# All 128 up blocks ahead of the first down block, in a fused decoder layer on one core

## The chip, the core and the metric

The kernel runs on one core of a Trainium2 chip. The core's engines work side by side, each through its own list of instructions in order: TensorE (PE) multiplies matrices, VectorE (DVE) and ScalarE (ACT) work element by element, GpSimd (POOL) issues the gathers here, and SyncE (SP) issues most of the other transfers between the chip's memory (DRAM) and the core's. ACT issues some transfers too. All transfers run on the same 16 DMA engines. The metric is the device time of one execution in microseconds (us).

## The reference, cut to what matters

The layer takes 512 tokens of width 1024 through a modulation, two kinds of attention with a projection, a LayerNorm, a PEER feed-forward part and a last LayerNorm. The change touches the PEER part alone, which is this:

```python
q = (hx @ w_pq).reshape(PEER_CHUNK, PEER_HEADS, 2, PEER_HALF)
sc = jnp.einsum('thpd,hpnd->thpn', q, sub_keys)
v_half, i_half = lax.top_k(sc, PEER_TOPK)          # 16 of 128 keys, twice per head
cand = v_half[:, :, 0, :, None] + v_half[:, :, 1, None, :]
cand_idx = i_half[:, :, 0, :, None] * N_KEYS + i_half[:, :, 1, None, :]
top_s, top_pos = lax.top_k(cand.reshape(...), PEER_TOPK)
idx = jnp.take_along_axis(cand_idx, top_pos, axis=-1)
g = jax.nn.softmax(top_s, axis=-1)
a = jax.nn.gelu(jnp.einsum('thkd,td->thk', u_tab[idx], hx), approximate=False)
return jnp.einsum('thk,thkd->td', (g * a).astype(hx.dtype), v_tab[idx])
```

Each token picks 8 x 16 of 16384 experts. An expert has a row of 1024 in `u_tab` and one in `v_tab`.

## The kernel before, in words

Tokens 0 to 127, and the first 64 tokens of the second tile for their `u` rows, go through **gathers**: POOL fetches one row of a table per token (`fetch`, L741, 512 KB for 128 rows), DVE multiplies it with the hidden row and sums (`dot`, L746), or adds a weighted `v` row to an accumulator (L782). There are 64 + 128 fetches of `u` and 128 of `v`, with five buffers. The generators `gather_part` and `gather_tile` hand out these steps, and a function `pull` takes steps worth so many nominal microseconds per block.

The rest of the tokens are computed **densely**, over 128 blocks of 128 experts. An **up block** (`u_block`, L802) loads 512 KB of `u`, splits it into a high part on ACT (L86) and a low part on DVE (L87), runs 24 matmuls over 320 tokens (L96 to L98 with the name `st`) and takes a GELU on ACT (L812). The result, `[128, 320]`, stays in a ring of 32 buffers (`a_r`) or goes to DRAM (`a_s`, then `a_d`, written by a transfer that ACT issues, L817) and is loaded again by SP later (`a_b`, L871). A **down block** (`v_block`, L858) loads 512 KB of `v`, splits it in the same way, multiplies the activation with the gate values of its experts (L874 on ACT, L875 on DVE), splits the product (L880, L881) and runs 18 matmuls of 512 columns into six accumulators in PSUM (L96 to L98 with the name `acc`).

**Gates.** Dense gate values come from the chosen indices: `make_g` builds one-hot tiles on DVE (L682, L684), scaled copies on ACT (`go`, L688), 8 small matmuls per step on PE in two groups of four (L692), and two copies of the PSUM results into a stage tile (L695), one on ACT and one on DVE. Two such steps fill a 1 MB stage that SP writes to `g_d` (L699). There are 48 steps for three tiles of 128 tokens. The down blocks read them back, 8 blocks at a time (`gl`, 1.5 MB, L853, issued by ACT, two buffers).

**Order.** Ahead of the gates comes the selection itself (`topk`, L553 to L660), also spread over the up blocks on DVE. The first loop runs `NB + NS` up blocks: `NB` = 32 kept in the ring and `NS` spilled to DRAM. In each of them some top-k work is pulled, `GRATE` gate steps are drained, and gather steps worth `RA` (before the weights of the second tile are ready) or `RB` (after) are pulled. The second loop runs 128 down blocks; as long as up blocks are left, each of its rounds runs one first and pulls 3.6 us of gather steps, afterwards 1.9 us. The down blocks take ring activations first, then the later up blocks' and the spilled ones last (`order`). At round 112 of 128 the ring is closed and the last stage's constants and inputs are loaded (L906 to L911); at round 116 the rest of the gathers is flushed. A scheduler places the instructions of each engine from this program order, so neighbouring blocks overlap and loads move ahead. Gather arithmetic is tied to the low-part splits by order (`paced`), so it can't run ahead of them.

SP's list is in order: a load that waits for a free buffer (three of `raw`) holds up all transfers behind it. The program also gives each transfer of SP and ACT one of eight completion counters (DMAHW0 to DMAHW7 in the order), in turn, and a transfer that gets a counter waits until the counter's last transfer has landed.

## Time and profile before

| | us |
|---|---|
| median of 3 runs | 1595.51 (1591.92 to 1604.62) |
| the profiled execution | 1601.17 |
| its span in the profile | 1599.4 |

| engine | busy us | share of the span |
|---|---|---|
| PE (matmul) | 1459.3 | 91% |
| DVE | 1309.6 | 82% |
| ACT | 782.3 | 49% |
| POOL | 486.7 | 30% |

The transfers moved 438.30 MB, 274 GB/s over the span. The mean granted TensorE clock was 0.959 of full speed. A busy share is an average over stages, so it is read per stage: the block loops' first weight split starts on DVE at 351.3 us, the 43rd at 640.75 us, the first product of a down block is made at 846.61 us, the last matmuls of an up block start at 1185.3 us, and the last gather step starts at 1443.84 us and takes 1.28 us.

### The profile page before, as it was taken

What the parts mean: (1) busy time and instruction counts of PE and PEld (TensorE: products, weight loads), DVE (VectorE), ACT (ScalarE), POOL (GpSimd) and SP (SyncE); (2) the same over time, 40 slices, a digit from 0 to 9 for tenths busy, and PEclk for the clock granted to TensorE, in tenths of its full rate; (3) what the DMA queues carried; (4) which work ended last, traced back from release to release, by engine and by line L of the source; (5) the groups of instructions that cost most, each with busy time, mean ns of one, the idle gap of its engine ahead of it and who ended that gap; (6) DMA issues with size and microseconds to landing.
All of it is one profiled execution on the core that took longest, in us unless ns stands there. A gap on an engine that the chain in (4) does not pass through costs nothing.

```text
span 1599.4 us, 22711 instructions
## 1 busy us (share of the span) xinstructions
PE 1459.3 (91%) x7837; PEld 1272.5 (80%) x7837; DVE 1309.6 (82%) x2654; ACT 782.3 (49%) x1475; POOL 486.7 (30%) x338
## 2 busy tenths in 40 slices
PE   6999898998688888999998989999999997899996
PEld 5777776888677778899997879999988885678884
DVE  7897665999899899988966888898889895778566
ACT  2565533335256668898963434443343342334340
POOL 0000000000543333752224655565545563430000
PEclk9999898999898899999998999999999997999998
DMA  8855443222877678998999999999989999998751
GB/s 303 290 189 186 152 165 112 79 80 80 302 252 254 229 259 297 316 365 319 326 366 341 368 365 363 366 368 378 364 315 369 349 352 353 334 336 268 225 174 53
DMA packets 173334, 438.30 MB, mean 274 GB/s; under 512 B 14562, under 2 KB 79458, under 8 KB 170019
## 3 DMA queue, kind: packets, MB, share of 16 engines
q1 hardware_dynamic: 69666, 234.72, 41.2%
q0 software_dynamic: 46080, 167.79, 29.0%
q10 hardware_dynamic: 57472, 34.35, 7.3%
q8 instruction: 61, 1.00, 0.2%
q14 instruction: 55, 0.44, 0.1%
HBM read 397.45 MB, written 39.33 MB: 273 GB/s over the span
## 4 chain that ended last, share of the span: by engine, by line
PE 49%; DMA 14%; issue 14%; DVE 13%; POOL 4%; ACT 4%; SPq 0%; POOLq 0%; DVEq 0%; ACTq 0%
DMA gl<-g_d 7%; PE acc L97 7%; PE acc L98 7%; PE acc L96 7%; PE bank L96 4%; PE bank L97 4%; PE bank L98 4%; POOL gb L741 4%; PE st L98 3%; PE st L96 3%; PE st L97 3%; DVE lo L87 2%; PE acc L692 2%; DMA gb<-u_tab,ei 2%; DVE gb L746 2%
## 5 line engine op out<-in xcount | busy, mean ns | idle before, releaser
L86 ACT CAST hi<-raw 128x1024 fp32r<-128x1024 f32 x286 | 299.2, 1050 | 278.5 <-DMA raw<-v_blk 71.8
L87 DVE TENSOR_TENSOR lo<-raw,hi 128x1024 fp32r<-128x1024 f32 x286 | 348.0, 1219 | 80.7 <-ACT hi L86 79.0
L96 PE MATMUL st<-h2h,hi 128*128 128x320 f32 x1024 | 330.5, 323 | 33.0 <-ACT hi L86 33.0
L98 PE MATMUL st<-h2h,lo 128*128 128x320 f32 x1024 | 328.3, 321 | 23.0 <-DVE lo L87 22.8
L97 PE MATMUL st<-h2l,hi 128*128 128x320 f32 x1024 | 325.3, 318 | 0.0
L97 PE MATMUL acc<-lo,wh 128*128 128x512 f32 x768 | 306.1, 399 | 17.6 <-DVE lo L87 17.0
L96 PE MATMUL acc<-hi,wh 128*128 128x512 f32 x768 | 304.3, 396 | 11.3 <-ACT hi L86 11.1
L98 PE MATMUL acc<-hi,wl 128*128 128x512 f32 x768 | 303.4, 395 | 0.0
L741 POOL DMA_INDIRECT gb<-u_tab,ei x128 | 204.1, 1595 | 229.0 <-DVE gb L746 213.0
L746 DVE SCALAR_TENSOR_TENSOR gb<-gb,h2n 128x1024 f32<-128x1024 f32 x192 | 231.0, 1217 | 17.3 <-DMA gb<-u_tab,ei 9.6
L741 POOL DMA_INDIRECT gb<-v_tab,ei x128 | 183.9, 1437 | 193.2 <-DVE acc L782 176.3
L96 PEld LDWEIGHTS st<-h2h,hi 128*128 128x128 f32 x1024 | 200.5, 196 | 39.0 <-ACT hi L86 37.3
L98 PEld LDWEIGHTS st<-h2h,lo 128*128 128x128 f32 x1024 | 199.6, 195 | 29.1 <-DVE lo L87 28.9
L97 PEld LDWEIGHTS st<-h2l,hi 128*128 128x128 f32 x1024 | 200.1, 195 | 1.5
L97 PEld LDWEIGHTS acc<-lo,wh 128*128 128x128 f32 x768 | 147.0, 191 | 52.2 <-DVE lo L87 21.4
L688 ACT ACTIVATE go<-oh,iT 128x128 f32<-128x128 bf16 x384 | 169.0, 524 | 33.9 <-DVE oh L682 26.9
L96 PEld LDWEIGHTS acc<-hi,wh 128*128 128x128 f32 x768 | 147.0, 191 | 43.5 <-ACT hi L86 12.8
L741 POOL DMA_INDIRECT gb<-u_tab,eip x64 | 88.8, 1387 | 280.3 <-DVE cand L555 148.7
L98 PEld LDWEIGHTS acc<-hi,wl 128*128 128x128 f32 x768 | 147.2, 192 | 30.9
L782 DVE SCALAR_TENSOR_TENSOR acc<-gb,w,acc 128x1024 f32<-128x1024 f32 x127 | 162.3, 1278 | 2.1 <-DMA gb<-v_tab,ei 2.0
L880 ACT CAST wh<-w 128x384 fp32r<-128x384 f32 x128 | 65.4, 513 | 177.1 <-PE acc L97 106.6
L104 POOL TENSOR_TENSOR rs_r<-rs_v,mhalf 128x1 f32<-128x1 f32 (+1 forms) x12 | 9.3, 775 | 399.8 <-DVE rs_v L102 364.2
(214 smaller groups left out, 2049.4 us busy)
## 6 DMA issues: line engine op xcount, KB each, us to landing
raw<-u_T SPq DMA_DIRECT2D x128, 512.0 KB
raw<-v_blk SPq DMA_DIRECT2D x128, 512.0 KB
wada<-w_adaT SPq DMA_DIRECT2D x48, 512.0 KB
g_d<-stage SPq DMA_DIRECT2D x24, 1024.0 KB
gl<-g_d ACTq DMA_DIRECT2D x16, 1536.0 KB
a_d<-a_s ACTq DMA_DIRECT2D x56, 160.0 KB
a_b<-a_d SPq DMA_DIRECT2D x56, 160.0 KB
raw<-w_pqT SPq DMA_DIRECT2D x16, 512.0 KB
```

What stands on the lines that cost most here:

```text
L86: nc.scalar.copy(hi, src)
L87: split.last = nc.vector.tensor_sub(lo, src, hi.bitcast(F32))
L96: nc.tensor.matmul(ps, lh, rh, start=first, stop=False)
L97: nc.tensor.matmul(ps, lh, rl, start=False, stop=False)
L98: nc.tensor.matmul(ps, ll, rh, start=False, stop=last)
L104: nc.gpsimd.tensor_tensor(r, v, mhalf.to_broadcast([P, n]), op=OP.pow)
L688: nc.scalar.activation(go[:, i, :], oh0[:, :, i], AF.Copy, scale=iT[:, 2, t0 + i:t0 + i + 1])
L692: nc.tensor.matmul(ps[:, i * P:(i + 1) * P], oh1[:, 4 * u + i, :], go[:, 4 * u + i, :], start=True, stop=True)
L741: nc.gpsimd.indirect_dma_start(out=b, out_offset=None, in_=A[tab], in_offset=bass.IndirectOffsetOnAxis(ap=idx[:, j:j + 1], axis=0))
L746: paced(nc.vector.scalar_tensor_tensor(b, b, 1.0, h2n, op0=OP.mult, op1=OP.mult, accum_out=acc))
L782: paced(nc.vector.scalar_tensor_tensor(acc0, b, w0[:, j:j + 1], acc0, op0=OP.mult, op1=OP.add))
L880: nc.scalar.copy(wh, w)
```

## The change

The first loop runs all 128 up blocks (`NB + NS` = 128), with 96 activations instead of 56 by way of DRAM; the second loop runs down blocks alone. `GRATE` falls from 0.8 to 0.52 gate steps per up block, `RA` from 2.2 to 1.7, `RB` rises from 1.3 to 1.9, and a down block's gather steps go from 3.6 (beside an up block) or 1.9 us to 1.6 us. Both stage copies of a gate step are on ACT. The tile for reloaded activations has four buffers instead of two.

```diff
-NS = 56
-GRATE = 0.8
+NS = 96
+GRATE = 0.52
...
-RA = 2.2
-RB = 1.3
+RA = 1.7
+RB = 1.9
...
-                    (nc.scalar.copy if u == 0 else nc.vector.tensor_copy)(
+                    nc.scalar.copy(
                         stage[:, :, w:w + 4].rearrange("p i t -> p t i"), ps.rearrange("p (t i) -> p t i", t=4))
...
-            a = vp.tile([P, TU], F32, name="a_b", tag="a_b", bufs=2)
+            a = vp.tile([P, TU], F32, name="a_b", tag="a_b", bufs=4)
             dma(a, a_d[e - NB])
...
             u_block(n + NB + NS)
             c2 = pull(gt, c2 + 3.6)
         else:
-            c2 = pull(gt, c2 + 1.9)
+            c2 = pull(gt, c2 + 1.6)
```

DVE, in the up blocks where top-k and gate steps overlap. Before (`lo` is a weight split, `gb,dots` a gather product, `oh` the one-hot tiles, `eq` top-k work, `stage` the PSUM copy):

```order
L645 TENSOR_TENSOR eq<-ab,lev 128x2048
L682 TENSOR_TENSOR oh_4857<-iTb,iota_3470 128x1024
L648 TENSOR_TENSOR eq<-eq,ixx 128x2048
L684 TENSOR_TENSOR oh_4859<-iT,iota 128x1024
L746 SCALAR_TENSOR_TENSOR gb,dots_3801<-gb,h2n 128x1024 x2
L695 COPY stage<-acc 128x4x128
L87 TENSOR_TENSOR lo<-raw,hi 128x1024
L651 TENSOR_TENSOR eq<-eq 128x8x128
L682 TENSOR_TENSOR oh_4925<-iTb,iota_3470 128x1024
L651 TENSOR_TENSOR eq<-eq 128x8x64
L684 TENSOR_TENSOR oh_4927<-iT,iota 128x1024
```

The same engine in the changed kernel, also in the up blocks with top-k and gate steps (`tv`, `tp`, `cand` are top-k work):

```order
L682 TENSOR_TENSOR oh_4524<-iTb,iota_3510 128x1024
L684 TENSOR_TENSOR oh_4526<-iT,iota 128x1024
L746 SCALAR_TENSOR_TENSOR gb,dots_3841<-gb,h2n 128x1024
L87 TENSOR_TENSOR lo<-raw,hi 128x1024
L553 MAX tv<-cand 128x8
L746 SCALAR_TENSOR_TENSOR gb,dots_3841<-gb,h2n 128x1024
L554 MAX_INDEX tp<-tv,cand 128x8
L87 TENSOR_TENSOR lo<-raw,hi 128x1024
L555 MATCH_REPLACE cand<-tv,cand 128x80
L682 TENSOR_TENSOR oh_4648<-iTb,iota_3510 128x1024
```

The copy from PSUM is gone from DVE, a gate step comes with about every second split, and fewer products stand between two splits. Counted between the first and the 43rd split of the block loops: 64 products, 20 gate steps and 19 copies before; 51, 14 and none now. The last gather step stands after 223 splits before (128 up and 95 down blocks) and after 232 now (128 and 104).

ACT, where gate steps meet spilled up blocks (`hi` is a weight's high part, `a_s` the GELU result, `a_d` its transfer to DRAM). Before:

```order
L688 ACTIVATE go<-oh_7914,iT 128x128 x8
L86 CAST hi<-raw 128x1024
L812 ACTIVATE a_s<-st 128x320
L695 COPY stage<-acc 128x4x128
L817 DMA a_d_125<-a_s 128x320
L688 ACTIVATE go<-oh_7976,iT 128x128 x8
L86 CAST hi<-raw 128x1024
```

ACT in the changed kernel:

```order
L688 ACTIVATE go<-oh_6673,iT 128x128 x5
L812 ACTIVATE a_s<-st 128x320
L86 CAST hi<-raw 128x1024
L817 DMA a_d_108<-a_s 128x320
L695 COPY stage<-acc 128x4x128 x2
L688 ACTIVATE go<-oh_6777,iT 128x128 x7
L812 ACTIVATE a_s<-st 128x320
L86 CAST hi<-raw 128x1024
L817 DMA a_d_109<-a_s 128x320
```

Both copies of a gate step now stand in ACT's list, where each waits for PE's small matmuls.

SP at the end of the gate steps (`raw` is a block's weights, `a_b` a reloaded activation, `g_d` a full stage). Before:

```order
L699 DMA g_d<-stage 128x2048
L92 DMA raw<-u_T 128x1024
L871 DMA a_b<-a_d_83 128x320
L871 DMA a_b<-a_d_84 128x320
L92 DMA raw<-u_T 128x1024 x5
L92 DMA raw<-v_blk 128x1024
L92 DMA raw<-u_T 128x1024
```

SP in the changed kernel:

```order
L699 DMA g_d<-stage 128x2048
L92 DMA raw<-u_T 128x1024
L871 DMA a_b<-a_d_83 128x320
L871 DMA a_b<-a_d_84 128x320
L871 DMA a_b<-a_d_85 128x320
L871 DMA a_b<-a_d_86 128x320
L92 DMA raw<-u_T 128x1024 x11
L92 DMA raw<-v_blk 128x1024 x33
L906 DMA g2r<-g_d 128x1024
```

Before, loads of `u` and `v` take turns from here on, for 40 rounds; now the last 11 `u` loads stand together and 33 `v` loads follow. The other 92 reloads of activations come one for about each later `v` load.

## Rows read from the trace of the kernel before

**Rows 1.** Windows by stage: stretch and length, then busy us (instructions) of each engine.

```profile
core 0: us, PE busy (x) PEld busy (x) DVE busy (x) ACT busy (x) POOL busy (x), PEclk, DMA share, GB/s
351.30:640.70 289.40, 236.99 (x1400) 217.74 (x1399) 266.16 (x738) 174.77 (x294) 94.32 (x68) 0.92 0.68 234
640.70:819.80 179.10, 175.09 (x1269) 171.54 (x1269) 160.65 (x202) 165.34 (x326) 73.45 (x41) 1.00 0.93 335
...
878.10:1183.70 305.60, 297.72 (x1630) 268.46 (x1629) 262.81 (x354) 121.32 (x201) 166.54 (x115) 0.99 0.98 360
1183.70:1311.00 127.30, 126.92 (x565) 105.08 (x564) 116.80 (x136) 50.76 (x90) 73.52 (x49) 1.00 0.99 359
1311.00:1445.10 134.10, 113.70 (x441) 89.20 (x440) 97.75 (x116) 42.33 (x75) 49.62 (x35) 0.89 0.96 339
1445.10:1599.40 154.30, 140.24 (x613) 114.50 (x612) 99.81 (x149) 51.55 (x93) 2.20 (x4) 0.97 0.56 177
```

**Rows 2.** Windows again, the whole stretch between two of those borders.

```profile
640.70:1445.10 804.40, 762.47 (x4216) 682.67 (x4216) 672.51 (x849) 399.48 (x721) 382.44 (x253) 0.97 0.97 350
```

**Rows 3.** Groups by line: operation, shapes, count, busy us, mean ns, idle before.

```profile
L86 ACT CAST hi<-raw 128x1024 fp32r<-128x1024 f32 x286 | 299.2, 1050 | 278.5 <-DMA raw<-v_blk 71.8 <-PE bank L97 71.0 <-PE st L97 50.7
L746 DVE SCALAR_TENSOR_TENSOR gb<-gb,h2n 128x1024 f32<-128x1024 f32 x192 | 231.0, 1217 | 17.3 <-DMA gb<-u_tab,ei 9.6 <-DMA gb<-u_tab,eip 5.9 <-issue 1.6
L684 DVE TENSOR_TENSOR oh<-iT,iota 128x1024 f32<-128x1024 f32 x48 | 58.3, 1214 | 0.0
L695 DVE COPY stage<-acc 128x512 f32<-128x512 f32 x48 | 50.7, 1056 | 18.2 <-PE acc L692 18.1
L682 DVE TENSOR_TENSOR oh<-iTb,iota 128x1024 bf16<-128x1024 bf16 x48 | 32.6, 682 | 4.3 <-ACT go L688 4.2
L812 ACT ACTIVATE a_s<-st 128x320 f32<-128x320 f32 x56 | 24.2, 434 | 16.1 <-PE st L98 8.8 <-DMA g_d<-stage 7.3
```

**Rows 4.** DMA queues: SP's (q1), POOL's (q0), ACT's (q10).

```profile
q1 hardware_dynamic: 69666, 234.72, 41.2%
q0 software_dynamic: 46080, 167.79, 29.0%
q10 hardware_dynamic: 57472, 34.35, 7.3%
```

**Rows 5.** Timeline of PE in an up block and in a down block.

```profile
750.11 0.31 PE L98 MATMUL st<-h2h,lo 128*128 128x320 f32 x1
...
752.45 0.31 PE L96 MATMUL st<-h2h,hi 128*128 128x320 f32 x1
...
1299.75 0.39 PE L96 MATMUL acc<-hi,wh 128*128 128x512 f32 x1
...
1300.88 0.39 PE L98 MATMUL acc<-hi,wl 128*128 128x512 f32 x1
```

**Rows 6.** Chain of waits: start, us, what; one gate step, one load of gates.

```profile
493.11 1.80 PE acc L692 x16
...
1309.91 29.56 DMA gl<-g_d
```

**Rows 7.** Windows again, two of 40 or 80 us.

```profile
720.00:800.00 80.00, 79.15 (x565) 76.71 (x564) 70.64 (x88) 74.22 (x149) 18.52 (x16) 1.00 0.89 323
1160.00:1200.00 40.00, 40.00 (x209) 35.32 (x209) 33.08 (x37) 16.58 (x28) 17.52 (x13) 1.00 0.88 315
```

**Rows 8.** Page, 40 slices of the span: what the DMA engines moved.

```profile
GB/s 303 290 189 186 152 165 112 79 80 80 302 252 254 229 259 297 316 365 319 326 366 341 368 365 363 366 368 378 364 315 369 349 352 353 334 336 268 225 174 53
```

**Rows 9.** Timeline of DVE: the wait for the first load of gates.

```profile
846.61 0.49 DVE L875 TENSOR_TENSOR w<-a_r,gl 128x320 f32<-128x320 f32 x1 [15.69 <-DMA gl<-g_d]
```

**Rows 10.** Waits of SP's queue from 1183 to 1445 us: total, times, longest.

```profile
SPq L911 <- DMA gl<-g_d: 21.9, 1, 21.9
SPq L92 <- DMA gl<-g_d: 19.6, 2, 10.6
...
SPq L871 <- DMA gl<-g_d: 11.0, 1, 11.0
```

## The prediction, made before the changed kernel was run

> **What bounds the kernel now.** I read the windows by stage first, since the busy shares of the page mix stages with different limits, and cut them where the block loops start, where the 43rd weight split stands, and where the gathers end [rows 1]. From 351.3 to 640.7 us DVE is busy 266 of 289 us while the DMA engines stand at 0.68 and the granted clock at 0.92: top-k, gate one-hots, copies and gather products share one engine, and PE waits for its splits. From 640.7 to 1445.1 us the DMA share is 0.97 over 804 us at 350 GB/s, and PE is busy 762 us as well [rows 2]. Two resources are nearly full there. Which one decides in a piece of it is seen in smaller windows: from 720 to 800 and from 1160 to 1200 us PE is full and the DMA share is only 0.89 and 0.88 [rows 7]; from 1311 to 1445 us the DMA share is 0.96, and PE has fallen to 114 of 134 us and the clock to 0.89 [rows 1]. After the gathers PE alone decides.
>
> PE's price per block comes from the spacing of its matmuls, not from their length, since they overlap: 16 steps take 2.34 us in an up block, so 0.146 x 24 = 3.51 us, and five steps take 1.13 us in a down block, so 0.226 x 18 = 4.07 us [rows 5]. A gate step's 8 matmuls leave 16 rows in the trace, 1.80 us [rows 6].
>
> The price of a transfer comes from the queues: share times the span of 1599.4 us over the bytes [rows 4]. SP's queue needs 2.81 us per MB (41.2%, 234.72 MB), POOL's 2.76, ACT's 3.40. So a 0.524 MB block load costs 1.47 us of all 16 engines, a gather 1.45, a spilled activation (0.164 MB) 0.56 to write and 0.46 to read, a gate load (1.573 MB) 5.35, a 1.05 MB stage 2.95.
>
> **The change, first stretch (to the 43rd split).** By the order of instructions 13 gather products, 19 PSUM copies and 6 gate steps leave DVE's list between those two splits. By their rows [rows 3]: 13 x 1.217 = 15.8, 19 x 1.056 = 20.1, and 6 x (0.682 + 1.214) = 11.4 us. Together 47.3 us come off a stretch in which DVE decides. The copies and the half of the products do not vanish: 20.1 us of copies go to ACT, the products and gate steps to later blocks. ACT was busy 175 of 289 us [rows 1], so it takes them; it reads PSUM in order between its splits, so I leave 3 us for DVE waiting for it. The stretch comes to 245 us, 44 less. Bounds: 230 if the copies' own waits for PE (18.1 us over all of them [rows 3]) go too, 260 if ACT's list holds up the splits.
>
> **Second stretch (43rd split to the last gather).** Here the transfers decide, and the change adds some:
> - 40 more spilled activations: 40 x 0.56 = 22.4 us.
> - Their reload: 97 products with gates stand ahead of the last gather step before, 25 of them on reloaded activations (order: 72 others first); now 106, of which 74 (32 others first). 49 x 0.46 = 22.5 us.
> - 13 gathers that left the first stretch: 13 x 1.45 = 18.9 us.
> - 6 gate steps that left it, three stages: 3 x 2.95 = 8.9 us.
> - Nine more down blocks ahead of the last gather step (223 splits before, 232 now): 9 x 1.47 = 13.2, and about one gate load more, 6 us.
>
> That is 92 us on top of 0.97 x 804.4 = 780 us of DMA time [rows 2], so 872 us. PE has 86 x 3.51 + 104 x 4.07 + 34 x 1.80 = 786 us to do in it, DVE even less per block than before, so the transfers decide nearly throughout, and the two windows in which PE held them back [rows 7] should go. At which share do the engines then run? The long windows with a full queue show 0.98 and 0.99 [rows 1], and the last one 0.96. I take 0.99, since two of the added buffers keep SP's reloads from waiting: 872 / 0.99 = 880 us. Bounds: 872 at 1.00, 899 at the old 0.97.
>
> ACT in this stretch: from 640.7 to 819.8 us it was busy 165 us for 36 up blocks and 28 gate steps [rows 1]. Less 36 x (1.050 + 0.434) [rows 3] that is 4.0 us per step with one copy. Now 66 blocks with 34 steps of two copies make 66 x 1.48 + 34 x 5.05 = 270 us, against 66 x (1.47 + 0.56) + 98 x 1.45 + 17 x 2.95 = 326 us of transfers (the order has 98 products there). So ACT's added copies cost nothing here; if the transfers were free they would still fit under PE's 293 us.
>
> The start of the gate loads stays: ACT issues the first one when the last stage has landed, and DVE waited 15.7 us for it [rows 9]. The order has the same sequence, only 33 up blocks later, so it is priced in the share.
>
> **Third stretch.** From the last gather step to the end 154.3 us passed, bound by PE [rows 1]. Nine down blocks less are left: 154.3 - 9 x 4.07 = 117.7 us.
>
> **Sum.** 351.3 + 245 + 880 + 117.7 = 1594 us of span, against 1599.4. The profiled execution is 1.8 us longer than its span, so 1595.8 against 1601.2; that execution lies 5.7 us above the median of 1595.5, so the forecast for the median is **1590 us**: what DVE gains at the start and what is no longer left at the end (81 us together) is given back to the transfers (76 us). About 1% (16 us) is what a measurement here can tell from no change, so the forecast counts as no change, at 0.50; its own range, with shares of 0.98 to 1.00 and 240 to 250 us for the first stretch, is 1577 to 1604.
>
> **A rule of the skill on the ceiling.** The busiest slice of 40 us moved 378 GB/s, and the long full windows 359 and 360 [rows 1, 8]. The Trainium skill, page "Perfetto Trace Analysis", section "Engine Utilization", gives about 435 GB/s as the ceiling of a single active core, some 120% of 358. If the transfers never held PE up, its 786 us and the 16 us wait [rows 9] would be the second stretch, and the time 1512 us. By that rule it could come near this. No slice of this trace comes near it while loads are waiting, so I give that 0.02, within the first rival.
>
> **Rivals.**
> *The queues stay full (0.25).* The first stretch loses the copies' waits too and falls to 230 us, and the second runs at 1.00: 351.3 + 230 + 872 + 117.7, with the same 3.9 us taken off, is 1567 us. For it: DVE had almost no idle time to begin with, and the stalls between 1311 and 1445 us came with two reload buffers. Against it: no long window showed more than 0.99.
>
> *Gate loads block SP's queue (0.18, slower).* From 1183 to 1445 us SP stood 52.5 us in four waits for a gate load to land [rows 10], because a block's load or a reload has to take over the completion counter of a gate load that takes 29.6 us [rows 6]. Behind it stand the next weights and activations. The 25 down blocks of that last window took 134.1 us, 5.36 each, against 4.07 for PE [rows 1]. Before, about 25 blocks ran with reloads and gathers together; now it is 72. Their transfers alone are 1.47 + 0.46 + 0.67 + 1.33 x 1.45 = 4.53 us per block (1.33 gather steps are 1.6 us at the program's 1.2), 4.57 at 0.99. At 5.36 the 72 blocks would cost 57 us more: 1647 us; if half of it comes through, 1618. It decides once a gate load takes longer than SP needs for its next eight transfers, some four blocks or 18 us. Against it: fewer gathers per block (1.33 against 1.9 / 1.2 = 1.58), and four reload buffers instead of two.
>
> *ACT becomes the bound of the up blocks (0.07).* With both copies and the write issues in its list, each behind a wait, a block of the 66 would take 5.3 us instead of 4.95: 23 us, 1613 us. Against it: 93% busy was possible between 720 and 800 us [rows 7], and 270 of 326 us is 83%.
>
> That the change does not do what it says is excluded by the order: all up blocks' loads stand ahead of the down blocks'.
>
> **Numbers.** Faster by over 1% (below 1579.6): most of the first rival and the low edge of the forecast's own range, 0.27. Slower (above 1611.4): the second rival, half of the third, and a little of the forecast's upper edge, 0.22. Within: 0.51. The range takes in the first rival and half of the second's price: 1562 to 1620, which leaves out about 0.2.
>
> **What would show it.** In the changed profile the 43rd split of the block loops should come near 596 us, with no copy from PSUM on DVE; from there to the last gather step the DMA share should be 0.98 to 1.00 at about 355 GB/s, with PE below it and the last gather step near 1476 us; the last 24 down blocks should run at 4.07 us each. It would be wrong if the 43rd split does not move (another engine than DVE decided), if PE is full and the DMA share is below 0.95 after it (the price of transfers is too high), or if SP's waits for gate loads grow to well over 100 us and the clock falls in the down blocks (second rival).

## The result, and the profile after

The changed kernel takes 1550.43 us (median of 4 runs, 1547.79 to 1554.21), the kernel before 1597.22 beside it: a ratio of 0.9706, 95% interval 0.966 to 0.9751. The forecast was 1590 us and no change, with a range from 1562. The kernel is 47 us faster, and the time lies 12 us below the range.

The profiled execution took 1551.68 us, its span is 1549.9 us. Its windows by stage are cut at the first split of the block loops, the 43rd, the 109th, the 129th (the first down block's), the 161st, the last gather step and the end; the first, the 43rd, the last gather step and the end are also borders in [rows 1] and [rows 2]. The row at the bottom is the whole stretch from the 43rd split to the last gather step.

```profile
core 0: us, PE busy (x) PEld busy (x) DVE busy (x) ACT busy (x) POOL busy (x), PEclk, DMA share, GB/s
345.70:588.90 243.20, 206.84 (x1291) 193.97 (x1290) 222.29 (x682) 155.44 (x243) 79.67 (x56) 0.95 0.68 236
588.90:884.00 295.10, 292.69 (x2101) 290.12 (x2100) 252.23 (x333) 262.87 (x475) 146.29 (x99) 1.00 1.00 386
884.00:976.00 92.00, 77.82 (x518) 77.16 (x518) 63.90 (x90) 39.01 (x64) 37.45 (x30) 0.91 1.02 390
976.00:1105.00 129.00, 127.76 (x568) 105.25 (x567) 116.04 (x151) 53.78 (x96) 63.45 (x44) 1.00 1.00 363
1105.00:1429.60 324.60, 304.05 (x1293) 246.46 (x1292) 261.97 (x313) 120.46 (x214) 129.92 (x92) 0.96 1.01 359
1429.60:1549.90 120.30, 106.56 (x465) 86.65 (x463) 80.27 (x121) 37.97 (x67) 2.20 (x4) 0.96 0.50 157
588.90:1429.60 840.70, 802.33 (x4474) 718.99 (x4473) 694.14 (x884) 476.12 (x847) 377.12 (x265) 0.98 1.00 373
```

Against before: the first stretch went from 289.4 to 243.2 us (46 less), the second from 804.4 to 840.7 (36 more), the end from 154.3 to 120.3 (34 less). The block loops also began 5.6 us earlier, at 345.7; in the runs below that border lies between 345 and 352 us whatever the kernel, so this is scatter. Read the second row first: over 66 up blocks PE is busy 293 of 295 us and the DMA engines stand at 1.00, and they move 386 GB/s. Before, the long stretches of [rows 1] showed 359 and 360, and the fullest one of this length that I find, from 870 to 1165 us, moved 367 at a share of 1.00 (its row stands further down).

The page's line of GB/s in 40 slices answers to [rows 8]:

```profile
GB/s 312 289 182 200 130 212 103 83 85 92 250 239 283 238 310 375 357 408 394 416 342 390 405 362 409 382 379 346 340 385 342 368 372 355 363 337 362 233 171 48
```

Four slices are above 400 GB/s, the highest at 416; the highest before was 378. The four lie in the up blocks. The queues, whole span, answer to [rows 4] (packets, MB, share):

```profile
q1 hardware_dynamic: 75426, 241.28, 43.0%
q0 software_dynamic: 46080, 167.79, 28.9%
q10 hardware_dynamic: 63232, 40.90, 8.7%
```

Share times span over bytes gives 2.76, 2.67 and 3.30 us per MB, where [rows 4] gave 2.81, 2.76 and 3.40. Every queue's price fell a little; SP's and ACT's queues move more, POOL's the same. The groups by line that answer to [rows 3]:

```profile
L695 ACT COPY stage<-acc 128x512 f32<-128x512 f32 x96 | 98.2, 1102 | 1.0 <-PE acc L692 0.9
L812 ACT ACTIVATE a_s<-st 128x320 f32<-128x320 f32 x96 | 41.6, 435 | 23.2 <-PE st L98 12.7 <-DMA g_d<-stage 10.5
```

All 96 copies are on ACT, with 1 us of waits where DVE's 48 had waited 18. Waits for gate loads remain in two places: DVE waits for the first one (answers to [rows 9]), and SP's queue over the whole span (as [rows 10]: total, times, longest):

```profile
925.29 0.49 DVE L875 TENSOR_TENSOR w<-a_r,gl 128x320 f32<-128x320 f32 x1 [17.63 <-DMA gl<-g_d]
```

```profile
SPq L871 <- DMA gl<-g_d: 54.9, 6, 14.5
SPq L92 <- DMA gl<-g_d: 42.7, 5, 12.5
SPq L911 <- DMA gl<-g_d: 20.0, 1, 20.0
```

### The profile page after: what moved, and what is told of

It is laid out like the page before. It is cut to its first block, busy times and chain, and to the rows that moved or that the text cites. A ratio compares the mean times of both kernels' runs of the same rounds, so it can differ in the third digit from the quotient of the medians.

```text
span 1549.9 us, 22874 instructions
## 1 busy us (share of the span) xinstructions
PE 1432.2 (92%) x7837; PEld 1254.3 (81%) x7837; DVE 1267.8 (82%) x2606; ACT 826.1 (53%) x1523; POOL 466.8 (30%) x338
## 4 chain that ended last, share of the span: by engine, by line
PE 47%; issue 14%; DMA 13%; DVE 11%; POOL 8%; ACT 5%; POOLq 0%; SPq 0%; DVEq 0%; ACTq 0%
POOL gb L741 8%; PE acc L97 7%; PE acc L98 7%; PE acc L96 7%; DMA raw<-v_blk 5%; PE bank L96 5%; PE bank L97 4%; PE bank L98 4%; DMA gl<-g_d 3%; DMA raw<-u_T 3%; DVE lo L87 3%; PE st L96 2%; PE st L98 2%; PE st L97 2%; ACT hi L86 2%
## 5 line engine op out<-in xcount | busy, mean ns | idle before, releaser
L96 PE MATMUL st<-h2h,hi 128*128 128x320 f32 x1024 | 326.3, 319 | 27.6 <-ACT hi L86 27.6
L98 PE MATMUL st<-h2h,lo 128*128 128x320 f32 x1024 | 322.0, 316 | 17.5 <-DVE lo L87 17.5
L97 PE MATMUL st<-h2l,hi 128*128 128x320 f32 x1024 | 321.7, 314 | 0.0
L741 POOL DMA_INDIRECT gb<-u_tab,ei x128 | 183.4, 1433 | 196.5 <-DVE gb L746 182.1
L96 PEld LDWEIGHTS st<-h2h,hi 128*128 128x128 f32 x1024 | 196.5, 192 | 31.2 <-ACT hi L86 31.2
L98 PEld LDWEIGHTS st<-h2h,lo 128*128 128x128 f32 x1024 | 196.0, 192 | 20.5 <-DVE lo L87 20.5
L97 PEld LDWEIGHTS st<-h2l,hi 128*128 128x128 f32 x1024 | 196.3, 192 | 0.0
L692 PE MATMUL acc<-go,oh 128*128 128x128 f32 x768 | 108.5, 284 | 7.3 <-ACT go L688 7.1
```

Of the source, the lines that this page charges most:

```text
L96: nc.tensor.matmul(ps, lh, rh, start=first, stop=False)
L97: nc.tensor.matmul(ps, lh, rl, start=False, stop=False)
L98: nc.tensor.matmul(ps, ll, rh, start=False, stop=last)
L692: nc.tensor.matmul(ps[:, i * P:(i + 1) * P], oh1[:, 4 * u + i, :], go[:, 4 * u + i, :], start=True, stop=True)
L741: nc.gpsimd.indirect_dma_start(out=b, out_offset=None, in_=A[tab], in_offset=bass.IndirectOffsetOnAxis(ap=idx[:, j:j + 1], axis=0))
```

## The experiments

Each ratio is against the kernel before, timed on the same chip beside it. Four questions were put: what each part of the change is worth, whether transfers or PE set the pace of the up blocks, the same for the down blocks, and what a better version needs.

### Parts of the change, one at a time

**Copies alone** (the kernel before, both stage copies on ACT).

```diff
-                    (nc.scalar.copy if u == 0 else nc.vector.tensor_copy)(
+                    nc.scalar.copy(
```

> The kernel before with one part of the change: both PSUM copies of a gate step on ACT. By the order its first 42 splits have no copy on DVE, two gate steps more (22) and one product more (65). Theory P (after the 43rd split the matmuls are the bound, the transfers' busy share is not): the first stretch shrinks by 19 x 1.056 - 2 x 1.9 - 1.2 = 15 us, the second by two gate steps of PE, 3 us; 1577 to 1584 us. Theory T (the transfers are the bound there, each byte has its price): 15 us in the first stretch and 4 us less of transfers after it, 1575 to 1582. This run only tells what the copies are worth, not the two theories apart.

Measured: 1591.86 us, ratio 0.9977 (0.9955 to 0.9999), a gain of 4 to 6 us. The first stretch shrinks to 276 us, but the next 36 up blocks, with 0.8 gate steps each, take 191 instead of 179 us. PE's work per block is the same as before and only ACT's list has grown, so it is ACT that decides there now (its busy time is the fourth of the engines'):

```profile
623.00:814.00 191.00, 186.83 (x1315) 179.94 (x1314) 135.65 (x169) 187.35 (x351) 49.78 (x39) 1.00 0.89 311
```

Neither expectation had seen that: the copies only pay with fewer gate steps per block.

**Order alone** (the kernel before, with all up blocks first).

```diff
-NS = 56
+NS = 96
```

> The kernel before with the new order alone (all 128 up blocks first, 96 spilled activations; gate steps at 0.8, gathers at 2.2 and 1.3, then 1.9 per down block, one stage copy on DVE, two reload buffers). Theory S: the up blocks stay at PE's pace and move some 335 GB/s, since neither gathers nor gate steps change; 40 more activations are written and read again, 13 MB or some 35 us, and the first stretch stays at 289 us; the last gather step stands after 231 splits instead of 223, which gives some 20 us back: 1605 to 1630. If the order itself is the gain (up blocks apart from gate loads move 386 instead of 360 GB/s): 1560 to 1585.

Measured: 1637.34 us, ratio 1.0282 (1.0251 to 1.0313): 42 us slower. The up blocks run as before:

```profile
635.00:813.00 178.00, 174.44 (x1264) 170.89 (x1263) 160.12 (x199) 164.53 (x325) 74.00 (x41) 1.00 0.92 336
```

So the order is no gain in itself. Theory S had the sign and the pace of the up blocks; its range ended 7 us lower.

**Order and gate steps back** (the changed kernel).

```diff
-NS = 96
-GRATE = 0.52
+NS = 56
+GRATE = 0.8
```

> The changed kernel with 56 spilled activations and 0.8 gate steps per up block as before, so 40 up blocks run beside down blocks again; copies on ACT, the pulls and four reload buffers stay as changed. First stretch: 51 products and 22 gate steps, so 8 steps x 1.9 = 15 us more on DVE than in the changed kernel. Theory P: those 8 steps leave PE's list in the second stretch (14 us less there), the spills there were free: 1546 to 1560 us. Theory T: 40 writes and about 40 reads of spilled activations less in the second stretch, 40 x 0.56 + 40 x 0.46 = 41 us, and 4 stages less, 12 us: 1505 to 1525 us. A third theory, that up and down blocks side by side slow the transfers (360 GB/s there before, 400 in the changed kernel's up blocks): 1570 to 1585 us.

**Gate steps back, order kept** (the changed kernel).

```diff
-GRATE = 0.52
+GRATE = 0.8
```

> The changed kernel with 0.8 gate steps per up block again, everything else kept: the steps end some 30 up blocks earlier. Theory S (a stretch in which PE or ACT decides leaves transfers undone, and its busy share hides that): the first stretch gets 8 more gate steps, 8 x 1.9 = 15 us; the next 36 up blocks run at ACT's pace, 191 us as in the kernel with the old order and both copies on ACT, against 158, and move some 335 GB/s at a share of 0.93 to 0.96, so that some 25 us of transfers are left for later: 1578 to 1595. By the price of the prediction (busy share is the work that is done): only 5% of 191 us, 10 us, are lost besides the 15, and part of them is won back: 1562 to 1575. If the place of the gate steps does not matter: 1548 to 1556.

Measured: 1581.43 us (ratio 0.9904, 0.9879 to 0.9928) and 1586.43 us (0.9952, 0.9927 to 0.9977). The first lies where the third theory had it, but not for its reason: the second keeps the new order and is as slow. The two differ in `NS` alone, and the old order is not the slower one. What the new order buys may be room: at 0.52 steps per block the 48 steps need 92 up blocks, and before only 88 stood ahead of the first down block. No run has the old order at a lower rate, so this is not shown. With the new order the rate is worth 36 us. In the second kernel, the first stretch and the 36 up blocks after it:

```profile
348.00:620.00 272.00, 228.20 (x1411) 210.82 (x1409) 238.19 (x699) 192.43 (x318) 78.81 (x56) 0.94 0.65 231
620.00:812.00 192.00, 186.00 (x1297) 179.94 (x1297) 150.81 (x197) 186.46 (x350) 74.66 (x53) 0.98 0.94 341
```

Eight gate steps more cost 29 us in the first stretch, 3.6 each, where the prediction priced one at 1.90 on DVE. DVE is busy 16 us more, which is that price; it also sits idle 13 us more, and its waits for ACT (19 against 11 us) and for PE's small matmuls (10 against 6) make up nearly all of that. In the second row ACT decides, and the transfers that the engines don't get to (341 GB/s against 386) are left for later.

**Gather pulls back** (the changed kernel).

```diff
-RA = 1.7
-RB = 1.9
+RA = 2.2
+RB = 1.3
...
-            c2 = pull(gt, c2 + 1.6)
+            c2 = pull(gt, c2 + 1.9)
```

> The changed kernel with the gather pulls of before (2.2 and 1.3 per up block, 1.9 per down block). By the order 64 instead of 51 products stand in the first stretch and 13 instead of 14 gate steps: 13 x 1.217 - 1.9 = 14 us more there. 134 instead of 149 products stand ahead of the 109th split, so more gathers are left for the down blocks. Theory P: plus 14 us, and plus 0 to 20 us for the gate loads' waits in the down blocks, since PE was not held up by transfers in the up blocks: 1560 to 1585 us. Theory T: 13 gathers less after the 43rd split, 13 x 1.4 = 18 us back: 1540 to 1552 us.

Measured: 1601.14 us, ratio 1.0022 (1.0003 to 1.004), outside of both expectations: the pulls are worth 51 us. This is the run that explains most. Its windows are the first stretch, the same 66 up blocks, and the 103 down blocks up to its last gather step (104 in the changed kernel):

```profile
350.00:604.00 254.00, 210.25 (x1269) 197.40 (x1269) 235.77 (x705) 152.11 (x236) 93.10 (x68) 0.92 0.71 249
604.00:902.00 298.00, 292.95 (x2094) 290.23 (x2093) 221.71 (x280) 264.51 (x481) 89.95 (x72) 0.99 0.94 340
988.00:1480.00 492.00, 450.14 (x1869) 360.36 (x1868) 399.18 (x503) 175.16 (x307) 227.17 (x159) 0.95 0.99 354
```

The 66 up blocks take 298 us, though they carry 27 gathers less than the changed kernel's (POOL 72 against 99 instructions): PE has the same work. The gathers that were not pulled there come in the down blocks, which take 492 instead of 454 us, and the first stretch grows by 11 us through 13 more products on DVE, with one gate step less (by the order of instructions). A gather beside an up block is free until the DMA engines are really full; beside a down block it costs at least its transfer: 38 us for 22 gathers (counted in the two orders of instructions), 1.7 us each, where the time of POOL's queue in this stretch comes to 1.4 us per gather.

**One copy back on DVE** (the changed kernel).

```diff
-                    nc.scalar.copy(
+                    (nc.scalar.copy if u == 0 else nc.vector.tensor_copy)(
```

> The changed kernel with one of the two stage copies of a gate step back on DVE. 12 of them fall into the first stretch, to the 43rd split. If the copies count there as the prediction had it: 12 x 1.056 = 13 us and about as much again for their waits for PE, so a first stretch of 256 to 268 us instead of 243; in the next 66 up blocks DVE gets 35 x 1.056 = 37 us on its 252 of 295, which still fits: 1562 to 1578. If DVE's place in the first stretch comes from the fewer gather products and gate steps alone: the stretch stays below 250 and the whole at 1548 to 1558.

Measured: 1563.76 us, ratio 0.9774 (0.9733 to 0.9816). The first stretch takes 254 us, 11 more for 12 copies, near the 13 that their own durations give; waits for PE beside them, which the expectation also counted, do not show. The copies count where the prediction had them.

**Two reload buffers again** (the changed kernel).

```diff
-            a = vp.tile([P, TU], F32, name="a_b", tag="a_b", bufs=4)
+            a = vp.tile([P, TU], F32, name="a_b", tag="a_b", bufs=2)
```

> The changed kernel with two buffers for reloaded activations instead of four. If the transfers decide in the down blocks, SP's queue has other loads to send and the buffers change little: 1546 to 1560. If reloads wait for their buffers, and behind them the weights (SP is in order), 104 blocks lose 0.1 to 0.3 us each: 1560 to 1580.

Measured: 1574.91 us, ratio 0.9872 (0.9838 to 0.9907): four buffers are worth 24 us, as the second expectation had it. The 104 down blocks take 481 us, and SP has a new wait, for an earlier reload to land:

```profile
979.00:1460.00 481.00, 439.74 (x1865) 354.69 (x1865) 378.94 (x463) 173.03 (x310) 201.42 (x136) 0.97 0.96 340
```

```profile
SPq L871 <- DMA a_b<-a_d: 37.6, 16, 4.4
```

The engines still show 0.96 while SP holds work back; the rate, 340 against 360 GB/s, tells it.

### What sets the pace of the up blocks

**Each spilled activation written twice** (the changed kernel).

```diff
             nc.scalar.dma_start(a_d[e - NB], acts[e])
+            nc.scalar.dma_start(a_x[e - NB], acts[e])
```

> The changed kernel with each of the 96 spilled activations written to DRAM twice, to two places: 15.7 MB more writes, all beside up blocks. In the changed kernel's up blocks from 589 to 884 us the DMA engines stand at 0.99 and PE is busy 293 of 295 us. Theory T (the transfers decide there): at the 2.73 us per MB of ACT's queue in that window (9.6% of 295 us for 10.36 MB) 54 of the writes there cost 24 us, all after the 43rd split 38 us: 1575 to 1595 us. Theory P (PE decides there, the transfers only keep up): nothing to 10 us, 1548 to 1562. Theory W (a write runs beside reads and is nearly free): as P, but then one more read must cost, which the next kernel tells.

Measured: 1597.34 us, ratio 1.0006 (0.9982 to 1.0029). T's range ended 2 us lower; it had counted 54 of the writes in this stretch, where ACT's queue shows 63 in the changed kernel (10.36 MB of 0.164 each). The 66 up blocks take 323 us, 28 more, at the same rate:

```profile
591.00:914.00 323.00, 300.90 (x2106) 295.03 (x2105) 250.96 (x332) 267.15 (x477) 139.15 (x97) 0.97 1.00 387
```

In this window SP's queue has waits that the changed kernel's up blocks don't have, for the spilled writes to land: 102 us in 34 waits, the largest of them

```profile
SPq L93 <- DMA a_x<-a_s: 56.1, 15, 6.7
SPq L93 <- DMA a_d<-a_s: 31.9, 13, 5.0
```

**One more read per spilled block.**

```diff
+            more = ring.tile([P, TU], F32, name="more", tag="more", bufs=2)
+            dma(more, A["u_tab"][e * P:(e + 1) * P, 0:TU])
```

> The changed kernel with one more read of 164 KB from DRAM, on SP, for each of the 96 spilled up blocks (not used by anything). Theory T: at 2.50 us per MB of SP's queue in the window 589 to 884 us, 35 us for the 86 reads after the 43rd split: 1575 to 1595. Theory P: 1548 to 1562. Theory W: as T here, while the second write costs nothing.

Measured: 1566.34 us, ratio 0.9793 (0.9734 to 0.9853), and it tells nothing on the question: the reads depend on nothing, and all 96 were issued before 470 us, ahead of the up blocks meant; those took 295 us at 385 GB/s, as without the reads. So a read was tied to its block:

```diff
         keep(e)
+        if e >= NB + 6:
+            more = ring.tile([P, TU], F32, name="more", tag="more", bufs=2)
+            dma(more, a_d[e - NB - 6])
```

> The changed kernel with each spilled activation read back once more, six up blocks after it was written, by SP into a tile that nothing uses; the read waits for the write, so it can't run ahead of the up blocks as the extra reads of the earlier kernel did (its 96 reads were issued before 470 us, and the stretch from 605 to 900 us took the same 295 us as without them). Some 85 reads of 164 KB lie between the 43rd and the last up block. Theory T (the transfers are at their wall of some 387 GB/s beside the up blocks, as the second writes suggested with 387 GB/s and 28 us more): 54 reads or 8.8 MB add 23 us to the 66 up blocks and all of them 32 to 36 us: 1578 to 1592. Theory P (PE decides, and the second writes cost time through ACT's list, which issues them): 1548 to 1560, with 410 GB/s or more in that stretch.

Measured: 1607.58 us, ratio 1.0064 (1.0038 to 1.009), 16 us above T's range. The 66 blocks take 337 us, 42 more, and SP stands in a new wait, for the write that it reads back:

```profile
594.00:931.00 337.00, 310.43 (x2130) 301.80 (x2129) 252.78 (x333) 263.82 (x475) 135.58 (x99) 0.97 0.99 377
```

```profile
SPq L831 <- DMA a_d<-a_s: 177.5, 50, 8.3
```

More writes on ACT and more reads on SP both make the up blocks longer: by 28 us for 11.1 MB more and by 42 us for 13.2 MB more, which at 386 GB/s take 29 and 34. That fits a stretch in which the transfers are full at about 386 GB/s. It does not prove it: SP's list, which also brings the weights, was held up in both runs, and how much of the 28 and of the 42 us is this wait is not split.

**No middle product in the up blocks** (the changed kernel).

```diff
-            mm3(ps, hi[:, k, :], lo[:, k, :], h2h[:, k, T0U:], h2l[:, k, T0U:], k == 0, k == KB - 1)
+            nc.tensor.matmul(ps, hi[:, k, :], h2h[:, k, T0U:], start=(k == 0), stop=False)
+            nc.tensor.matmul(ps, lo[:, k, :], h2h[:, k, T0U:], start=False, stop=(k == KB - 1))
```

> The changed kernel without one of the three products of the up blocks (the high weights times the low hidden part, L97), which is left out; 8 matmuls of 24 less per up block, no transfer and no DVE or ACT work less. Theory P: PE saves 8 x 0.147 = 1.17 us per up block, 100 us over the 86 blocks after the 43rd split; the transfers become the bound at their best pace seen (about 405 GB/s), so 40 to 70 us are gained: 1480 to 1510 us. Theory T: the transfers stay the bound: 1540 to 1552 us.

Measured: 1570.87 us, ratio 0.9848 (0.9817 to 0.9878), slower than the changed kernel, which no theory had. The same 66 blocks:

```profile
589.00:897.00 308.00, 262.66 (x1601) 230.59 (x1602) 248.30 (x329) 267.48 (x478) 149.55 (x97) 0.98 0.99 376
```

A third of the up blocks' matmuls is gone (500 fewer in the window), and the blocks take 13 us more, at a DMA share of 0.99. That PE alone sets the pace of the up blocks falls with this. Why it is slower stays open: the scheduler also placed ACT's and DVE's lists differently, so it isn't PE's work alone that differs.

### What sets the pace of the down blocks

**Two gate loads instead of 16** (the changed kernel).

```diff
-            gls[order[n + GB]] = g_load(order[n + GB])
+            gls[order[n + GB]] = g_load(order[n + GB]) if n < GB else gls[order[n - GB]]
```

> The changed kernel with only the first two of the 16 loads of gate values; the later down blocks use them again, so 22 MB of reads and the right gate values are left out. In the down blocks ACT's queue moves packets of about 0.5 KB (15.51 MB in 30449 packets from 1105 to 1430 us) at 3.60 us per MB, and the whole moves 359 GB/s, against 386 in the up blocks. Theory T (transfers decide in the down blocks, and the gate loads are their dearest part): 13 loads of 5.7 us ahead of the last gather step, 74 us, come off until PE's 4.07 us per block decides: the 104 down blocks go from 454 us to 425 to 430, in all 1520 to 1530 us. Theory P (PE decides there too, with its own stalls): 1542 to 1554. If waits of SP's queue behind gate loads decide, those are gone as well: 1510 to 1525, with the DMA share well below 1.

Measured: 1521.01 us, ratio 0.9524 (0.9494 to 0.9554). PE is full in the 103 down blocks up to the last gather step, which take 418 us, 4.06 each, the prediction's price of 4.07 for PE:

```profile
977.00:1395.00 418.00, 416.68 (x1836) 343.69 (x1836) 377.72 (x460) 169.86 (x309) 226.69 (x136) 1.00 0.95 343
```

Theory T gave 1520 to 1530. The third reading, in which SP's waits behind gate loads decide, gave 1510 to 1525 with a share well below 1 (it is 0.95), and its range holds the time as well: those waits went from 101 us in the changed kernel's down blocks to none. So the run shows what the gate loads cost in all, some 32 us for the same 103 down blocks, and not by which way. The granted clock is 1.00 here and 0.96 in most of the changed kernel's down blocks. Again a share of 0.95 goes with a PE that decides.

**Gate values in another order in DRAM** (the changed kernel).

```diff
-    g_d = dram.tile([NTG, P, NKEY, TG], F32, name="g_d")
+    g_d = dram.tile([P, NKEY // GB, NTG, GB * TG], F32, name="g_d")
...
-            dma(g_d[(t - 1) * (P // TG) + tg], stage)
+            dma(g_d[:, :, (t - 1) * (P // TG) + tg], stage.rearrange("p (b i) t -> p b (i t)", i=GB))
...
-        nc.scalar.dma_start(gl, g_d.rearrange("g p i t -> p g (i t)")[:, :, e * TG:(e + GB) * TG])
+        nc.scalar.dma_start(gl, g_d[:, e // GB])
```

> The changed kernel with another order of the gate values in DRAM: a load of 1.57 MB is then one piece of 12 KB for each of 128 rows, and a stage is written in pieces of 0.5 KB, where before the stage was written in 8 KB pieces and the load read in pieces of 0.5 KB. Bytes, instructions and order stay. If the size of the pieces sets the price (ACT's queue 3.60 us per MB in the down blocks, against 2.7 of the others): 13 loads ahead of the last gather step fall from 5.7 to 4.2 us, 20 us less in the down blocks until PE decides there; the writes grow by as much, of which a third lies in the first stretch, where there is room: 1535 to 1550, with the 104 down blocks at 428 to 436 us instead of 454. If bytes alone count: no change in either part, 1546 to 1555. If small writes are dearer than small reads: 1560 to 1585.

Measured: 1559.73 us, ratio 0.9778 (0.9724 to 0.9832). The down blocks take 436 us, as T had it, and the 66 up blocks 314, 19 more:

```profile
595.00:909.00 314.00, 301.96 (x2140) 297.90 (x2139) 251.75 (x333) 263.91 (x475) 141.96 (x100) 0.99 1.02 369
1001.00:1437.00 436.00, 427.37 (x1867) 350.23 (x1866) 376.71 (x463) 173.80 (x310) 218.00 (x137) 0.99 0.99 376
```

The small pieces moved from the loads to the writes, and what was gained beside the down blocks was lost beside the up blocks; T had hidden more of that price, and its range ended 10 us lower. The price of the pieces can be read from ACT's queue in the down blocks, which is nearly the gate loads alone (packets, MB, share), in the changed kernel from 976 to 1430 us and here from 1001 to 1437:

```profile
q10 hardware_dynamic: 40428, 20.87, 16.4%
```

```profile
q10 hardware_dynamic: 2321, 20.96, 11.9%
```

The same bytes cost 16.4% of 454 us or 3.57 us per MB in packets of 0.5 KB, and 11.9% of 436 us or 2.48 in packets of 9 KB. SP's waits for gate loads in the down blocks fell with it, from 101 us to 2, so the 18 us gained there are not split between price and waits either.

### A better version

**Slower gathers in the down blocks** (the changed kernel): the last gather step comes eleven down blocks later.

```diff
-            c2 = pull(gt, c2 + 1.6)
+            c2 = pull(gt, c2 + 1.45)
```

> The changed kernel with gather steps worth 1.45 instead of 1.6 us per down block: the last gather step stands after 243 splits instead of 232, so ten more down blocks share the same gathers and the end has ten less at PE's pace alone. Theory T: the stretch to the last gather step grows by the loads of ten or eleven blocks, 11 x (1.3 + 0.45) = 19 us, the end shrinks by 11 x 4.07 = 45 us, 20 to 26 us in all: 1525 to 1535. Theory P: PE's work is the same and nothing moves, 1545 to 1555.

Measured: 1541.28 us, ratio 0.9648 (0.962 to 0.9676). Down blocks to the last gather step, and the end:

```profile
981.00:1467.00 486.00, 473.40 (x2062) 387.47 (x2061) 399.89 (x493) 191.57 (x343) 197.14 (x136) 0.99 1.00 356
1467.00:1540.00 73.00, 59.10 (x255) 47.08 (x253) 56.06 (x89) 19.45 (x34) 2.32 (x4) 0.93 0.38 124
```

The time lies between T's range and P's. The end shrinks by 47 us and the stretch ahead grows by 32, more than the 19 expected; that sum had left out the gate loads of the eleven blocks (1.4 of them at 5.7 us, 8 us), and 5 us stay unexplained. It lies some 9 us below the changed kernel's 1550; the two intervals overlap in part. Three variations of it added nothing that is clear of noise. With the last 32 up blocks in the ring, `RB` 2.1 and the same pull:

```diff
-RB = 1.9
+RB = 2.1
...
-            c2 = pull(gt, c2 + 1.6)
+            c2 = pull(gt, c2 + 1.45)
...
-        if NB <= e < NB + NS:
+        if e < NS:
...
-    order = list(range(NB)) + list(range(NB + NS, NKEY)) + list(range(NB, NB + NS))
+    order = [e for g in range(NKEY - GB, NS - 1, -GB) for e in range(g, g + GB)] + list(range(NS))
```

> A version that should beat the changed kernel: the last 32 up blocks stay in the ring instead of the first 32, so that 32 of the 96 spilled writes move ahead of the 43rd split, where the DMA engines stand at 0.55 to 0.78, and the first down blocks use the newest activations, so that their first product stands after 126 splits instead of 114, behind the wait for the first gate load; RB is 2.1 instead of 1.9 and a down block's gather steps 1.45 instead of 1.6, so that all 192 u products stand before the first down block (180 before). Theory T: 18 us of writes leave the full stretch, 12 gathers (1.35 us each) leave the down blocks for up blocks that now have the room, and half of the 17.6 us wait goes: 1515 to 1530. Theory P (PE decides in up blocks as well): only the wait and the gathers at the end, 1530 to 1542. If the faster pull overloads DVE (252 of 295 us and 10 more products of 1.22), 1545 or more.

Measured: 1547.23 us, ratio 0.9675 (0.9635 to 0.9716). The up blocks took 303 us, 8 more than the changed kernel's, and the down blocks 443, 11 less: gathers moved beside up blocks that were already full took their price with them. With that ring, the same pull and `RB` at 1.9:

```diff
-        if NB <= e < NB + NS:
+        if e < NS:
...
-            c2 = pull(gt, c2 + 1.6)
+            c2 = pull(gt, c2 + 1.45)
```

> A version that should beat the changed kernel: the last 32 up blocks in the ring instead of the first, and a down block's gather steps worth 1.45 instead of 1.6, with RB at 1.9 as in the changed kernel. The pull alone gave 1541. Theory T: 5 MB of writes move from the full stretch into the first one, 13 us, and part of the wait for the first gate load goes: 1525 to 1537. If the earlier writes collide there with what DVE and ACT do, or are not what decides: 1538 to 1545.

Measured: 1545.1 us, ratio 0.9692 (0.9656 to 0.9728). The writes that moved ahead gave nothing that can be seen. The same 66 up blocks moved 1.5 MB less than the changed kernel's and still took 295 us, with PE busy 292:

```profile
596.00:891.00 295.00, 291.91 (x2091) 288.93 (x2091) 250.93 (x331) 261.78 (x475) 140.93 (x98) 1.00 0.99 381
```

This bears on the pace of the up blocks too: fewer transfers alone did not shorten them. With the slower gathers and eight reload buffers:

```diff
-            a = vp.tile([P, TU], F32, name="a_b", tag="a_b", bufs=4)
+            a = vp.tile([P, TU], F32, name="a_b", tag="a_b", bufs=8)
```

> The version with gather steps worth 1.45 per down block (1541 us), with eight buffers for reloaded activations instead of four. Two instead of four cost 24 us, and then SP waited 47.6 us in 20 waits for an earlier reload to land. If that wait was the whole of it (in the changed kernel it is below the 4.6 us of the list's last row): no gain, 1538 to 1545. If the reloads still hold SP back at four (63.4 us in 46 waits for the product that frees a buffer): 1520 to 1535.

Measured: 1543.41 us, ratio 0.9619 (0.9583 to 0.9654). That is 5 us less by the medians' ratios than with four, within the intervals, and the down blocks to the last gather step take as long: no gain from more than four buffers is shown.

## Why the prediction was wrong

**First stretch: right.** 245 us forecast, 243.2 measured. The split of the 47 us into terms was fair in sum only: one undo each shows 11 us for 12 copies (20 had been counted for 19), 11 for 13 products with one gate step less (16 for the products), and 29 for eight gate steps (15 by the prediction's price). The gate steps were priced at half, since only DVE's busy time was counted and not its waits, and the others a little high; that the sum came out is partly luck.

**The end: right.** 117.7 us forecast, 120.3 measured, from the same split count.

**The down blocks: right.** The sum of transfers gave 4.53 us per block, 4.57 at a share of 0.99; the 72 blocks from 1105 us to the last gather step took 324.6 us, 4.51 each. The prices behind it erred both ways, and that the sum fits so closely is partly luck: in these blocks SP's queue took 2.70 us per MB and POOL's 2.66, less than the prediction's 2.81 and 2.76, and ACT's 3.57, more than its 3.40. The rival that gate loads block SP's queue did not come at its price of 5.36 us per block. Its sign did: SP's waits for gate loads grew from 71 us over the whole span (36.3, 21.9 and 12.9 in the same view of before) to 118, and the clock there was 0.96. The DMA engines stayed at 1.00, but the two kernels above that take these waits away (two gate loads, other order in DRAM) also shorten the down blocks, so a smaller price of the waits is not ruled out. The four reload buffers did what the prediction had them do: with two, the down blocks take 27 us more. That this is also the distance between its bounds of 872 and 899 us is chance.

**The up blocks: wrong, and this is the step that failed.** "Here the transfers decide", and for the 66 blocks "326 us of transfers". They took 295, with PE busy 293 of them, so the transfers did not decide alone. The bytes were right: its counts for the second stretch (40 writes and 49 reads of activations, 13 gathers, three stages, nine blocks, a gate load) make 30.8 MB, and 31.8 came (313.31 against 281.50). The price was not. It came from a queue's share of the whole span over its bytes, and the base of 780 us from a share of 0.97. Both take busy time for work done. SP's and POOL's queues beside the same up blocks, in two kernels: the changed one from 589 to 884 us, and the one with the gather pulls back from 604 to 902 us (packets, MB, share).

```profile
DMA packets 35197, 113.92 MB, mean 386 GB/s; under 512 B 3976, under 2 KB 12069, under 8 KB 33081
...
q0 software_dynamic: 14129, 51.48, 45.6%
q1 hardware_dynamic: 11938, 51.71, 43.8%
```

```profile
DMA packets 31790, 101.38 MB, mean 340 GB/s; under 512 B 3602, under 2 KB 11869, under 8 KB 29586
...
q1 hardware_dynamic: 12120, 52.75, 48.7%
q0 software_dynamic: 10344, 37.67, 35.5%
```

The second moves 11% fewer bytes in nearly the same time, yet SP's queue takes 48.7% of 298 us for 52.75 MB, 2.75 us per MB, and the first 43.8% of 295 us for 51.71 MB, 2.50. POOL's price falls from 2.81 to 2.61. Packets of the same mean size on the same queue took less time each at the higher rate; why is not shown. A share of 0.94 therefore was not 6% of room but 12%: 340 against 386 GB/s. The kernel before has the same reading in its own window from 640.7 to 819.8 us, 335 GB/s at 0.93 [rows 1], where PE was busy 175 of 179 us. Its 60.1 MB would take 156 us at 386 GB/s; by the share I had counted 167. Finer windows of the same trace already held the warning (columns as in [rows 1]):

```profile
694.40:716.80 22.40, 22.40 (x169) 22.40 (x168) 21.28 (x28) 20.52 (x42) 7.63 (x6) 1.00 1.03 415
870.00:1165.00 295.00, 287.12 (x1582) 259.62 (x1581) 257.11 (x350) 116.62 (x193) 167.93 (x117) 0.99 1.00 367
```

For 22 us the kernel before moved 415 GB/s. There SP's queue took 2.44 us per MB (51.3% of 22.4 us for 4.71 MB), against the 2.81 of the whole span.

By queue the 326 us (before the division by 0.99) come apart so: SP's queue had 147 and took 129, POOL's had 142 and took 135, ACT's had 37 and took 28. ACT's part has another cause than the share. Its price of 3.40 us per MB mixed the writes of activations with the gate loads, and beside up blocks, where ACT's queue carries the writes alone, they stood at 2.78 in the kernel before (640.7 to 819.8 us) and 2.74 in the changed one (588.9 to 884):

```profile
q10 hardware_dynamic: 5040, 5.74, 8.9%
```

```profile
q10 hardware_dynamic: 9101, 10.36, 9.6%
```

So the 880 us came to 840.7 in this way: the base of 281.5 MB at the 373 GB/s of the stretch is 755 us instead of 780; the added 30.8 MB cost 83 instead of 92; and the share was 1.00 instead of 0.99, 8 us. That is 42 us for a difference of 39, with 3 the other way for the extra MB. Since the 373 is measured, this divides the difference and does not explain the rate.

The Trainium skill has a rule for this, page "Perfetto Trace Analysis", section "Identifying the Most-Contended Engine": for DMA, go by the bytes moved against the peak and not by occupancy, which misleads with 16 engines. The trace agrees: 340 and 386 GB/s at 0.94 and 1.00. The prediction weighed the ceiling of about 435 GB/s that this page gives (section "Engine Utilization") and dismissed it for want of a slice of 40 us above 378; the 22 us at 415 in the same trace speak against that, and after the change the 39-us slices reach 416. The rate still fell short of the ceiling over any long stretch, and the up blocks' PE time, which I had as 293 us, was by then as long as the transfers'. The prediction's own sign for a price that is too high, a share below 0.95 with PE full, did not come: it was read from the share as well.

**The rivals.** "The queues stay full", at 1567 us, was nearest: its share of 1.00 came, its first stretch of 230 us did not, and it kept the wrong price. What stood against it, that no long window showed more than 0.99, came from where the windows were cut: 870 to 1165 us shows 1.00. ACT did not become the bound at 0.52 gate steps per block (263 of 295 us); at 0.8 with both copies it does, in three kernels.

**What the parts are worth.** Taking one part back from the changed kernel costs 51 us (gather pulls), 36 (gate rate), 24 (reload buffers) and 13 (copies) by the medians, and 50, 39, 27 and 11 by the ratios. The order alone, on the kernel before, costs 42. The parts don't add up to the 47 gained; parts that move the same limits would do this, but no run takes two of them back together.

**What stays open.** Which limit sets 386 GB/s in the up blocks and 360 in the down blocks: the 0.5 KB packets, or the waits that came with them, are part of the difference (376 with larger ones), not shown to be all of it. And whether PE or the transfers end last in the up blocks, where both are full: a third less of PE's work did not shorten them, nor did 1.5 MB less to move, while more to move made them longer.

## What to carry to other kernels

Read a stretch's room for transfers from the GB/s that the same mix reaches when it is pushed, not from the busy share of the DMA engines, which here stood at 0.89 to 0.95 while another engine decided. Put movable transfers beside stretches in which PE decides and take them out of stretches that transfers decide; the same gather cost nothing that shows in one and 1.7 us in the other. Price a queue's work where it will run: an average over the whole span mixes packets of different sizes. An order that costs time by itself may still pay with other rates beside it: test the two together and apart (here both orders stand side by side at 0.8 gate steps only).

## What was not expected of the hardware

In the up blocks a MB became cheaper at the higher rate: 2.75 to 2.50 us on SP's queue, 2.81 to 2.61 on POOL's, at 340 and 386 GB/s. In the down blocks only SP's did so: with two gate loads and with the other order in DRAM (343 and 376 GB/s) it stood at 2.95 and 2.72, POOL's at 2.60 and 2.61. Reads in packets of 0.5 KB cost 3.57 us per MB and in packets of 9 KB 2.48, for the same 21 MB; the Trainium skill's page "Perfetto Trace Analysis", section "DMA Optimizations", has small transfers below 2 KB as dear, and this agrees. Writing each activation twice cost 28 us for 11.1 MB more in the window, 2.5 us per MB with SP's waits for these writes in it, so here more writes did not ride free beside reads.
